# Attention scores by residue: near keys dense, far keys by position mod 4, two heads side by side in plain float32 products

## The chip, the cores and the metric

The kernel runs on one core of one Trainium2 chip. The metric is the device time of one execution in microseconds (us). The kernel before took 1199.07 us, the median of three runs (1199.07 to 1199.63). A difference of less than about 0.2% can't be told from none.

## What is computed

One layer of a decoder trunk: RMSNorm, one input projection, eight attention heads (this document's subject) and four HGRN2 heads side by side, an output projection, then a gated MLP with a short convolution, and a last RMSNorm. The sequence has 1024 positions, the model 1024 columns, an attention head 64. The part that the change touches:

```python
DILATED_PATTERNS = ((128, 1), (512, 4), (2048, 16))   # (window, dilation)

def dilated_attention(q, k, v):
    ...
    for window, dilation in DILATED_PATTERNS:
        o, m, l = dilated_branch(q, k, v, window, dilation)   # causal, keys at distance 0, d, 2d, ... up to window
        ...
    w = jnp.exp(ms - jnp.max(ms, axis=0, keepdims=True))
    den = jnp.sum(w * ls, axis=0)
    num = jnp.sum(w[..., None] * os_, axis=0)
    return (num / den[..., None])[:, :S]
```

The three branches are merged by their softmax denominators. So the whole is one softmax over the causal keys, in which a key counts as often as it stands in a branch: once for each distance up to 128, once more for each distance up to 512 that 4 divides, once more for each distance up to 2048 that 16 divides. Both kernels add the logarithm of that count to the score as a mask, and minus a huge number where the count is zero. Beyond a distance of 128 only distances that 4 divides have a count.

## The kernel before

**Number forms.** Most products run in a rounded float32 form (`F32R`). For accuracy the kernel splits an operand into a high part, rounded, and a low part, the rest, and adds up high x high, high x low and low x high: the dense projections are three products each. A weight piece of 128 x 512 comes by DMA on SP's queue (`Ring.fill`, line 66), ACT makes the high part (line 86), POOL or DVE the low part (line 88). The ring holds five split pieces and five raw ones.

**Stages.** First the norm sums and the projections of heads 0 and 1 and of the first values; then the attention stage, a loop over the heads; then HGRN, output projection, MLP. The attention stage does more than attention: a queue of other work (`Fill`, the projections of q and k of the next heads, of values and of HGRN's `iv`) is run in shares between the attention steps, by the microseconds that each step is said to cost. PE's instructions stand in the order in which the program writes them. The order on the other engines and in SP's DMA queue is made by a scheduler.

**Scores** (`score_steps`). For a head and a block of 128 queries, all causal keys: `n = 128 * (block + 1)` columns. The 64 numbers of a head fill half of the array's 128 rows, so the high part of q stands in rows 0 to 63 and its low part in rows 64 to 127 (`qs`), over the high part of k twice (`kh`); a second product with the low part of k (`kl`) over the high part of q completes it (lines 599, 600). `qk_half` makes `qs`, `kh` and `kl` out of the projection, for most heads by five SBUF-to-SBUF DMAs (line 568). DVE adds the mask and takes the row's minimum of the negated score (line 604), ACT takes the exponential and its sum (608), DVE the reciprocal (609), POOL scales (612).

**Values** (`value_steps`). Each 128 x 128 block of probabilities is transposed on TensorE (lines 627 to 634, tile `T`), split into a high part by ACT (637) and a low part by DVE (638), and multiplied with values that hold high and low parts side by side (646 to 650, tile `O`). An ACT copy and two DVE additions gather the output (654 to 657).

HGRN, later in the kernel, has a product that uses half of the array's columns (`psA`, lines 909 and 910): for a block of 128 positions the two chunks of 64 go to rows 0 to 63 and 64 to 127 of one PSUM bank, as plain float32 products.

Of the kernel before, what the change touches and what calls it, by code (L numbers as in the profile page):

```python
# [43 lines left out]
def f32(ap):  # L44
    return ap.bitcast(F32)
# [157 lines left out]
def hybrid_kernel(ctx: ExitStack, tc: tile.TileContext, xT, w_qk, w_tok, w_hg, w_out, w_up,  # L203
# [63 lines left out]
    want_tok("V1_0", 1)  # L267
    for h in (2, 3, 4):
        want(("qk", h), w_qk[h])
        want_tok(f"V1_{h - 1}", 1)  # L270
    want(("qk", 5), w_qk[5])
    want_iv(0)
    want(("qk", 6), w_qk[6])
    want_iv(1)
    want(("qk", 7), w_qk[7])
    want_iv(2)
    want_iv(3)
# [91 lines left out]
    TB = 3  # L369
# [156 lines left out]
    vs = {}  # L526
    iv = None
    if True:
        mask = at.tile([P, SEQ], F32, name="mask")
        nc.sync.dma_start(mask, amask)  # L530

        for hf in range(2):
            POOL.tensor_scalar(mask[:, halves[hf]], mask[:, halves[hf]], DH ** 0.5, 0.0, op0=ALU.mult, op1=ALU.add)
        NQ = 2
        kls = []
        for i in range(NQ):
            kl = at.tile([P, SEQ], F32R, name=f"kl{i}")
            POOL.memset(f32(kl[64:128]), 0.0)
            kls.append(kl)
# [3 lines left out]

        def qk_half(h, hf, last, tag="mm"):
            t = halves[hf]

            def evac(ps):
                if hf == 0:
                    qk[h] = (at.tile([P, SEQ], F32R, tag="qs", name=f"qs{h}", bufs=NQ),
                             at.tile([P, SEQ], F32R, tag="kh", name=f"kh{h}", bufs=NQ), kls[h % NQ])  # L550
                qs, kh, kl = qk[h]
                lo = at.tile([P, H2], F32R, tag="x", name=f"x{h}_{hf}")
                x = f32(lo)
                DVE.tensor_mul(x, ps, R1[:, t])
                if h == 0:
                    ACT.copy(qs[0:64, t], x[0:64])
                    ACT.copy(kh[64:128, t], x[64:128])
                    ACT.copy(kh[0:64, t], x[64:128])
                    DVE.tensor_sub(qs[64:128, t], x[0:64], f32(qs[0:64, t]))
                    DVE.tensor_sub(kl[0:64, t], x[64:128], f32(kh[64:128, t]))  # L560
                    return

                hi = at.tile([P, H2], F32R, tag="xh", name=f"xh{h}_{hf}")
                ACT.copy(hi, x)
                DVE.tensor_sub(lo, x, f32(hi))
                for dst, src in ((qs[0:64, t], hi[0:64]), (kh[64:128, t], hi[64:128]), (kh[0:64, t], hi[64:128]),
                                 (qs[64:128, t], lo[0:64]), (kl[0:64, t], lo[64:128])):
                    nc.sync.dma_start(f32(dst), f32(src))
            return dense(("qk", h), hf, evac, last, tag)
# [3 lines left out]

        def v_evac(g):
            def evac(t, ps):
                if g not in vs:
                    vs[g] = vtile([P, 8, 4, P], F32R, f"v{g}")
                dst = vs[g][:, t]
                src = ps[:, :256].rearrange("p (h e) -> p h e", h=4)
                ACT.mul(dst[:, :, 0:64], src, R1T[:, t : t + 1])  # L580
                DVE.scalar_tensor_tensor(dst[:, :, 64:128], src, R1T[:, t : t + 1], f32(dst[:, :, 0:64]),
                                         op0=ALU.mult, op1=ALU.subtract)
            return evac

        def score_steps(h, j):
            Ps = []
            qs, kh, kl = qk[h]
            for i in range(2):
                qb = 2 * j + i
                n = (qb + 1) * P  # L590
                Pt = at.tile([P, (5 + i + 2 * (j % 2)) * P], F32, tag=f"P{j % 2}{i}", name=f"P{h}_{qb}")
                st = at.tile([P, 16], F32, tag="st", name=f"st{h}_{qb}", bufs=8)
                Ps.append(Pt)
                cut = 320 if n == 640 else H2
                for k0 in range(0, n, cut):
                    w = min(n, k0 + cut) - k0
                    S = bank("s", f"S{h}_{qb}_{k0}")
                    q = qs[:, qb * P : (qb + 1) * P]
                    PE.matmul(S[:, :w], q, kh[:, k0 : k0 + w], start=True, stop=False)  # L599
                    PE.matmul(S[:, :w], q, kl[:, k0 : k0 + w], start=False, stop=True)  # L600
                    m = SEQ - n + k0

                    low = st[:, k0 // cut : k0 // cut + 1]
                    DVE.tensor_tensor_reduce(Pt[:, k0 : k0 + w], S[:, :w], mask[:, m : m + w], -(DH ** -0.5),  # L604
                                             st[:, 0:1] if k0 else BIG * 3,
                                             op0=ALU.add, op1=ALU.min, accum_out=low)
                    if k0 + w == n:
                        ACT.activation(Pt[:, :n], Pt[:, :n], AF.Exp, bias=low, scale=-1.0, accum_out=st[:, 2:3])  # L608
                        DVE.reciprocal(st[:, 3:4], st[:, 2:3])  # L609
                        for s0 in range(0, n, H2):  # L610
                            e = Pt[:, s0 : min(n, s0 + H2)]
                            POOL.tensor_scalar(e, e, st[:, 3:4], 1.0, op0=ALU.mult, op1=ALU.mult)  # L612
# [938 lines left out]
```

## Time and profile before

| | |
|---|---|
| median of the runs | 1199.07 us |
| span of the profiled execution | 1197.7 us |
| PE busy | 1186.0 us, 99% of the span |
| DVE busy | 938.7 us, 78% |
| ACT busy | 621.1 us, 52% |
| POOL busy | 300.4 us, 25% |
| first score product of attention | 40.1 us |
| first product of HGRN | 290.66 us |

The profile is of one execution; its span, from the first to the last instruction, is what sums are made against, and its median run time is 1.4 us above it. A timeline row gives start, duration, engine, line, operation, output and inputs, the part of the array used (rows * columns), the shape, and a count; matmuls overlap, so their durations are longer than their pitch. A row of groups gives the count, busy time and mean duration, and the idle time before it with what ended it. In the row of a stretch the busy times of PE, weight loads (PEld), DVE, ACT and POOL stand one after the other.

### The profile page before, as it was taken

Reading aid. Unit: us, or ns where it says so; the run is one execution under the profiler, and the core shown is the slowest. Engines: PE = TensorE matmul, PEld = TensorE weight load, DVE = VectorE, ACT = ScalarE, POOL = GpSimd, SP = SyncE. Lnnn points to the kernel's source line nnn. Section 1 sums busy time; section 2 is a strip of 40 time slices with the busy share of each in tenths; the row PEclk is TensorE's granted clock in tenths of the full one; section 3 lists DMA queues with packets and bytes.
Section 4 is the critical chain, followed back from the end, with each engine's and each line's share of the span. In section 5 each row is a group of like instructions: output and inputs, shape, how many; then the busy total and the mean of one; then the engine's idle time right before and its main releaser. Section 6 shows DMA issues by size and latency. Waiting matters only on the chain.

```text
span 1197.7 us, 17305 instructions
## 1 busy us (share of the span) xinstructions
PE 1186.0 (99%) x5854; PEld 995.9 (83%) x5854; DVE 938.7 (78%) x1762; ACT 621.1 (52%) x1203; POOL 300.4 (25%) x275
## 2 busy tenths in 40 slices
PE   9999999999999999999999999999999999999996
PEld 8988888888888888888888888888888888888886
DVE  7777675567878776485999889898888978957996
ACT  8666666667766554455543334343343444444553
POOL 2155446653001024322232222322232200000000
PEclk9999999999999999999999999999999999999998
DMA  7233333433102113441113322333223267435532
GB/s 264 53 96 103 100 104 104 133 105 100 48 33 62 60 57 120 138 140 60 53 62 114 118 80 98 119 115 121 87 92 115 97 234 238 153 97 157 169 104 91
DMA packets 77433, 131.56 MB, mean 110 GB/s; under 512 B 8480, under 2 KB 18976, under 8 KB 77344
## 3 DMA queue, kind: packets, MB, share of 16 engines
q1 hardware_dynamic: 66128, 110.59, 29.5%
q10 hardware_dynamic: 11216, 19.86, 4.3%
q8 instruction: 46, 0.75, 0.3%
q14 instruction: 43, 0.35, 0.1%
HBM read 97.65 MB, written 23.59 MB: 101 GB/s over the span
## 4 chain that ended last, share of the span: by engine, by line
PE 98%; DVE 1%; DMA 0%; POOL 0%; issue 0%; SPq 0%; ACT 0%; DVEq 0%
PE p L1152 11%; PE p L1150 11%; PE p L1151 11%; PE ds L1450 3%; PE ds L1449 3%; PE ds L1451 3%; PE po L1054 2%; PE po L1056 2%; PE po L1055 2%; PE da L1450 2%; PE da L1451 2%; PE da L1449 2%; PE O L646 2%; PE S L600 1%; PE S L599 1%; PE piv L513 1%
## 5 line engine op out<-in xcount | busy, mean ns | idle before, releaser
L88 POOL TENSOR_TENSOR wlo<-raww,whi 128x512 fp32r<-128x512 f32 x138 | 205.6, 1500 | 371.6 <-ACT whi L86 258.3
L86 ACT CAST whi<-raww 128x512 fp32r<-128x512 f32 x276 | 167.8, 617 | 191.7 <-DVE raww L120 62.1
L88 DVE TENSOR_TENSOR wlo<-raww,whi 128x512 fp32r<-128x512 f32 x139 | 99.1, 714 | 20.2 <-ACT whi L86 20.1
L86 ACT CAST whi<-r 128x512 fp32r<-128x512 f32 x70 | 43.6, 622 | 81.0 <-PE ds L1450 48.1
L612 POOL TENSOR_SCALAR P<-P,st 128x512 f32<-128x512 f32 (+2 forms) x96 | 57.9, 612 | 96.1 <-DVE st L609 76.9
L638 DVE TENSOR_TENSOR t<-T,t 128x512 fp32r<-128x512 f32 (+1 forms) x80 | 50.9, 636 | 17.5 <-ACT t L637 16.1
L88 DVE TENSOR_TENSOR wlo<-r,whi 128x512 fp32r<-128x512 f32 x70 | 48.2, 690 | 18.8 <-ACT whi L86 18.5
L1451 PE MATMUL ds<-fhi,wlo 128*128 128x512 f32 x160 | 62.2, 389 | 0.0
L1150 PE MATMUL p<-b1h,whi 128*128 128x512 f32 x160 | 62.2, 389 | 0.0
L1151 PE MATMUL p<-b1l,whi 128*128 128x512 f32 x160 | 62.2, 389 | 0.0
L1152 PE MATMUL p<-b1h,wlo 128*128 128x512 f32 x160 | 62.2, 389 | 0.0
L1449 PE MATMUL ds<-fhi,whi 128*128 128x512 f32 x160 | 62.2, 389 | 0.0
L1450 PE MATMUL ds<-flo,whi 128*128 128x512 f32 x160 | 62.2, 389 | 0.0
L608 ACT ACTIVATE P<-P,st 128x128 f32<-128x128 f32 (+3 forms) x64 | 49.7, 777 | 23.8 <-DVE st L604 23.2
L1179 ACT ACTIVATE cv<-cv 128x512 f32<-128x512 f32 x44 | 27.8, 632 | 62.0 <-DVE cv L1172 61.9
L1172 DVE SCALAR_TENSOR_TENSOR cv<-g,vec,cv 128x511 f32<-128x511 f32 (+2 forms) x92 | 56.1, 616 | 4.7 <-ACT cv L1169 3.7
L637 ACT CAST t<-T 128x512 fp32r<-128x512 f32 (+1 forms) x80 | 43.2, 540 | 29.5 <-PE T L631 26.4
L1423 POOL TENSOR_TENSOR facc<-facc,sqf 128x256 f32<-128x256 f32 x2 | 1.5, 738 | 223.6 <-ACT sqf L1422 223.6
L604 DVE CUSTOM_DVE_ANT_0 P<-S,mask 128x128 f32<-128x128 f32 (+3 forms) x64 | 35.5, 562 | 27.2 <-PE S L600 21.0
L88 DVE TENSOR_TENSOR flo<-rawf,fhi 128x512 fp32r<-128x512 f32 x70 | 48.3, 689 | 3.3 <-ACT fhi L86 3.2
L86 ACT CAST fhi<-rawf 128x512 fp32r<-128x512 f32 x70 | 43.2, 617 | 14.0 <-PE p L1152 5.0
L1449 PE MATMUL da<-fhi,whi 128*128 128x512 f32 x120 | 46.7, 389 | 0.0
(677 smaller groups left out, 3774.3 us busy)
## 6 DMA issues: line engine op xcount, KB each, us to landing
raww<-in_w_up_dram SPq DMA_DIRECT2D x88, 256.0 KB, 3.0
raww<-in_w_tok_dram SPq DMA_DIRECT2D x52, 256.0 KB, 2.8
rawf<-spT SPq DMA_DIRECT2D x40, 256.0 KB, 2.7
r<-in_w_down_dram SPq DMA_DIRECT2D x40, 256.0 KB, 3.4
raww<-in_w_hg_dram SPq DMA_DIRECT2D x32, 256.0 KB, 2.6
raww<-in_w_out_dram SPq DMA_DIRECT2D x32, 256.0 KB, 2.6
spB<-a ACTq DMA_DIRECT2D x30, 256.0 KB, 2.2
spT<-t ACTq DMA_DIRECT2D x30, 256.0 KB, 2.0
```

What stands on the lines that cost most here:

```text
L86: self.pin(self.high(hi[:, :w], raw))
L88: self.pin(low.tensor_sub(lo[:, :w], raw, f32(hi[:, :w])))
L608: ACT.activation(Pt[:, :n], Pt[:, :n], AF.Exp, bias=low, scale=-1.0, accum_out=st[:, 2:3])
L612: POOL.tensor_scalar(e, e, st[:, 3:4], 1.0, op0=ALU.mult, op1=ALU.mult)
L638: DVE.tensor_sub(t2[:, 1, :n], T[:, :n], f32(t2[:, 0, :n]))
L1150: PE.matmul(ps, hi[:, s], bhi, start=(start and n == 0), stop=False)
L1151: PE.matmul(ps, hi[:, s], blo, start=False, stop=False)
L1152: PE.matmul(ps, lo[:, s], bhi, start=False, stop=(stop and n == len(rhs) - 1))
L1172: DVE.scalar_tensor_tensor(dst, x, col(V_CW + j * NFF + f), dst, op0=ALU.mult, op1=ALU.add)
L1449: PE.matmul(ps[d], hi[:, s], ahi, start=(k == 0), stop=False)
L1450: PE.matmul(ps[d], hi[:, s], alo, start=False, stop=False)
L1451: PE.matmul(ps[d], lo[:, s], ahi, start=False, stop=(k == NPAIR - 1))
```

## The change

Three things change together, for the attention stage alone.

**Keys.** A block of 128 queries is now scored against near keys (its own block and the one before, at most 256 columns, dense) and far keys (all blocks before these). The queries of a block are stored in the order of their residue mod 4, 32 of each (`by_residue`); the 32 queries of residue r are scored against the far keys of residue r alone, read at a stride of four: four products of 32 queries by `32 * block` columns, which go to four groups of 32 PSUM rows. Far keys of other residues have a count of zero. A score row is thus at most 480 columns, where it was 1024. The mask is made anew in this order (`sel`, `scratch`, `mask`: POOL keeps each key either in the near or in the far part, and two trips through DRAM put the rows in the order of the residues).

**Number form and heads.** q, k, v and the probabilities are no longer split: the products are plain float32. Two heads stand side by side, head 2p in rows 0 to 63 and head 2p + 1 in rows 64 to 127 of `qp` and `kp`, and their products use half of the array's rows each, with a PSUM bank for each head. In the value products the heads use half of the array's columns each and go to the two halves of one bank.

**Values and order.** Values are kept once (`V`) for the near keys; they are also written to DRAM (`vd`), from where `load_far` reads them by residue for the far keys. The far probabilities are collected over a half of the sequence: `far_t` for the keys that all four blocks of the second half share, `tri` for the others. The loop runs over four pairs of heads and eight blocks: scores of the next block, a share of the fill, the transposes of this block, another share; after four blocks the value products. The ring's plan has the weights in the matching order.

```diff
-    for h in (2, 3, 4):
+    for h in (2, 3):
         want(("qk", h), w_qk[h])
-        want_tok(f"V1_{h - 1}", 1)
...
+    for i in (0, 1):
+        want_tok(f"V1_{i}", 1)
...
     def aside(i):
-        t = at.tile([P, 2, H2], F32R, tag="t", name=f"tw{i}", bufs=TB)
+        t = at.tile([P, 2, H2], F32R, tag="k0", name=f"tw{i}", bufs=2)
...
+        FAR, NEAR = 224, 256
+        nat = at.tile([P, SEQ], F32, tag="k0", name="nat", bufs=2)
...
+        nc.sync.dma_start(nat1[:, 0:NEAR], amask[:, SEQ - NEAR :])
+        nc.sync.dma_start(nat[0:32, 0:896], amask[0:P:4, 0:896])
...
+        nc.sync.dma_start(scratch[:, FAR:], sel[:, FAR:])
+        nc.sync.dma_start(scratch[0:32, 0:FAR], sel[0:32, 0:FAR])
+        for r in range(4):
+            nc.sync.dma_start(mask[32 * r : 32 * r + 32, FAR:], scratch[r:P:4, FAR:])
+            nc.sync.dma_start(mask[32 * r : 32 * r + 32, 0:FAR], scratch[0:32, 0:FAR])
...
+        def by_residue(ap):
+            return ap.rearrange("p (b l r) -> p b r l", l=32, r=4)
...
+                q4 = qp[r0 : r0 + 64, t].rearrange("p (b r l) -> p b r l", r=4, l=32)
+                DVE.tensor_mul(q4, by_residue(ps[0:64]), by_residue(R1[0:64, t]))
+                DVE.tensor_mul(kp[r0 : r0 + 64, t], ps[64:128], R1[64:128, t])
...
+                dst = V[:, t, 4 * g : 4 * g + 4]
+                ACT.mul(dst, ps[:, :256].rearrange("p (h e) -> p h e", h=4), R1T[:, t : t + 1])
+                nc.scalar.dma_start(vd[t * P : (t + 1) * P, 256 * g : 256 * g + 256], dst)
...
+        def load_far(p, kb):
...
+            src = vd[H2 * kb : H2 * (kb + 1), P * p : P * (p + 1)]
+            nc.sync.dma_start(far_v[p][:, kb], src.rearrange("(p r) e -> p r e", r=4))
...
+        def scores(p, b):
...
+            for e in range(2):
+                PE.matmul(S[e][:, far:n], qp[rows[e], b * P : (b + 1) * P], kp[rows[e], k0 : k0 + near],
+                          start=True, stop=True)
+            for r in range(4 if b else 0):
+                o = slice(32 * r, 32 * r + 32)
+                for e in range(2):
+                    PE.matmul(S[e][o, 0:far], qp[rows[e], b * P + 32 * r : b * P + 32 * r + 32],
+                              kp[rows[e], r : r + 4 * far : 4], start=True, stop=True)
...
+        def turn(p, b):
...
+                    PE.transpose(T[:, e, x], Ps[e][:, c : c + P], ident)
+            ACT.copy(d[:, :, x0:], T[:, :, x0:])
...
+                    PE.transpose(T[:, x, e], Ps[e][:, x * P : (x + 1) * P], ident)
...
+                DVE.tensor_copy(far_t[p][:, :, b - 4], T[:, 0])
...
+                DVE.tensor_copy(tri[b // 4][0:n, :, b % 4 - 1], T[0:n, parts - 1])
+
+        def values(p, hf):
...
+                        PE.matmul(O4[rows[e], i], V[:, b - 1 + x, 2 * p + e], t[:, e, x], start=(i == 0 and x == 1), stop=False)
...
+                        PE.matmul(O4[rows[e], :, q], v[:, 0, r, rows[e]], far_t[p][:, e, :, q], start=False, stop=False)
...
+                    PE.matmul(O4[rows[e], 1:, q], v[0:96, hf, r, rows[e]], tri[hf][0:96, e, :, q], start=False, stop=(r == 3))
...
+        for p in range(NH // 2):
+            work, us = beside[p]
+            fill.add(*work)
+            for b in range(8):
+                while ends:
+                    values(*ends.pop())
+                s = 8 * p + b + 1
+                if s < 32:
+                    scores(s // 8, s % 8)
+                fill.run(us / 16)
...
+                turn(p, b)
...
```

How the instructions move is seen at three places. The first is PE in the middle of the attention stage. Before, rows for block 3 of head 3 (`S` scores, `kh`/`kl` keys, `p__qk___4_0` a projection from the fill queue, `T` transposes):

```order
L599 MATMUL S_3_0_1756<-kh_1451,qs_1450 128x512
L600 MATMUL S_3_0_1756<-kl_206,qs_1450 128x512
L459 MATMUL p__qk___4_0_1747<-uhi,whi_1571 128x512
L461 MATMUL p__qk___4_0_1747<-ulo,whi_1571 128x512
L462 MATMUL p__qk___4_0_1747<-uhi,wlo_1572 128x512
L627 MATMUL T_0_0_1767<-ident,P_0_1605 128x128
L628 MATMUL T_0_0_1767<-ident,P_1_1617 128x128
L634 MATMUL T_0_0_1767<-ident,P_1_1617 128x128
```

In the changed program, block 3 of the second pair of heads (`S_3_0` and `S_3_1` are the two heads' banks):

```order
L460 MATMUL p__qk___4_1_1424<-uhi,whi_1266 128x512
L462 MATMUL p__qk___4_1_1424<-ulo,whi_1266 128x512
L463 MATMUL p__qk___4_1_1424<-uhi,wlo_1267 128x512
L610 MATMUL S_3_0_1457<-kp_840,qp_839 128x256
L610 MATMUL S_3_1_1458<-kp_840,qp_839 128x256
L615 MATMUL S_3_0_1457<-kp_840,qp_839 32x96
L615 MATMUL S_3_1_1458<-kp_840,qp_839 32x96
```

Two full-width products of one head have become two near products and eight far ones of two heads; the last two rows stand three more times, for the other residues. The second place is PE where value products stand. Before, one step of head 3:

```order
L646 MATMUL O_3_1629<-t_3_3_1695,v_439 128x512
L648 MATMUL O_3_1629<-t_3_3_1695,v_439 128x2x128
L459 MATMUL p__qk___4_1_1832<-uhi,whi_1571 128x512
L461 MATMUL p__qk___4_1_1832<-ulo,whi_1571 128x512
L462 MATMUL p__qk___4_1_1832<-uhi,wlo_1572 128x512
```

In the changed program, the first half of the first pair of heads (`pl` the transposed near probabilities, `vs` the values by residue):

```order
L669 MATMUL O_0_928<-pl_0_660,V 64x128 x2
L669 MATMUL O_0_928<-pl_1_758,V 64x128 x4
L669 MATMUL O_0_928<-pl_2_826,V 64x128 x4
L669 MATMUL O_0_928<-pl_3_897,V 64x128 x4
L676 MATMUL O_0_928<-tri_227,vs_548 64x3x32 x8
L610 MATMUL S_5_0_952<-kp_335,qp_334 128x256
L610 MATMUL S_5_1_953<-kp_335,qp_334 128x256
```

The value products, before spread between pieces of the fill, now stand together, with the scores of the next block right behind them. The third place is SP's DMA queue after the loads of x. Before:

```order
L530 DMA mask<-in_amask_dram 128x1024
L66 DMA raww_331<-in_w_tok_dram 128x512
L66 DMA raww_337<-in_w_tok_dram 128x512
L66 DMA raww_343<-in_w_tok_dram 128x512
L66 DMA raww_352<-in_w_tok_dram 128x512
```

In the changed program, from the load of the far mask on (`nat`; the near half has gone the same way a few rows ahead):

```order
L536 DMA nat<-in_amask_dram 32x896
L66 DMA raww_724<-in_w_qk_dram 128x512
L66 DMA raww_736<-in_w_qk_dram 128x512
L66 DMA raww_748<-in_w_qk_dram 128x512
L546 DMA scratch<-sel 32x224
L66 DMA raww_771<-in_w_tok_dram 128x512
L66 DMA raww_880<-in_w_tok_dram 128x512
L549 DMA mask<-scratch 32x224 x4
L596 DMA vs_548<-vd 128x4x128
L596 DMA vs_1160<-vd 128x4x128
L66 DMA raww_910<-in_w_tok_dram 128x512
L66 DMA raww_1042<-in_w_tok_dram 128x512
```

One load of the mask has become a chain through DRAM with weight loads in between, and the loads of the far values (`vs`) stand ahead of later weight loads. The five copies of each projected q and k half (line 568) are gone from the queue.

More of the change, by code (lines that the diff above doesn't have):

```diff
@@ L542, in hybrid_kernel @@
         qk = {}
+        def by_residue(ap):
+            return ap.rearrange("p (b l r) -> p b r l", l=32, r=4)
         def qk_half(h, hf, last, tag="mm"):
             t = halves[hf]
+            p, r0 = h // 2, 64 * (h % 2)
             def evac(ps):
[L548 to L568, printed above, removed]
+                if p not in qk:
+                    qk[p] = [at.tile([P, SEQ], F32, tag=x, name=f"{x}{p}", bufs=2) for x in ("qp", "kp")]
+                qp, kp = qk[p]
+                q4 = qp[r0 : r0 + 64, t].rearrange("p (b r l) -> p b r l", r=4, l=32)
+                DVE.tensor_mul(q4, by_residue(ps[0:64]), by_residue(R1[0:64, t]))
+                DVE.tensor_mul(kp[r0 : r0 + 64, t], ps[64:128], R1[64:128, t])
             return dense(("qk", h), hf, evac, last, tag)
@@ L572, in qk_block @@
             return [qk_half(h, 0, False), qk_half(h, 1, True)]
+        V = None
+        vd = drv.tile([SEQ, NH * DH], F32, name="vd")
         def v_evac(g):
             def evac(t, ps):
[L576 to L582, printed above, removed]
@@ L583, in v_evac @@
-            return evac
[L585 to L592, printed above, removed]
-                Ps.append(Pt)
[L594 to L612, printed above, removed]
-                    yield Ps
@@ L683, in iv_evac @@
             ACT.mul(iv[:, t], ps, R1T[:, t : t + 1])
-        lo4, hi4, all8 = range(4), range(4, 8), range(8)
+        all8 = range(8)
         v0 = [tok("V0", t, v_evac(0), t == 7, "mm" if t > 1 else "s") for t in all8]
@@ L709, in hybrid_kernel @@
         ring.on_vector += [(("out", 1, d), i) for d in range(NCT) for i in range(2)]
-        for Ps in score_steps(0, 0):
-            pass
+        scores(0, 0)
         fill.add(v0[3])
         fill.run()
+        load_far(0, 0)
         rms1(1)
@@ L719, in hybrid_kernel @@
         fill.run()
+        for g in pairs[1]:
+            next(g, None)
         ivs = [tok_pair(i, iv_evac) for i in range(4)]
[L721 to L730 removed]
@@ L764, in hybrid_kernel @@
-        while pending:
-            late_pv()
-        late_ends()
+        twos = [two("V1", i, v_evac(1)) for i in range(4)]
+        beside = [(v0[5:] + qk_block(2) + qk_block(3) + twos[:2], 39.3),
+                  (qk_block(4) + qk_block(5) + twos[2:], 31.4),
+                  (qk_block(6) + qk_block(7) + ivs[:1], 31.2),
+                  (ivs[1:], 31.2)]
+        ends = []
+        for p in range(NH // 2):
[8 more added lines that the diff above has]
+                fill.run(us / 16)
+                if b == 3:
+                    load_far(p, 1)
+                turn(p, b)
+                if b == 6 and p < 3:
+                    load_far(p + 1, 0)
+                if b == 7:
+                    fill.run()
+                else:
+                    fill.run(us / 16)
+                if b % 4 == 3:
+                    ends.append((p, b // 4))
@@ L767, in hybrid_kernel @@
+        values(*ends.pop())
+    drv_cm.__exit__(None, None, None)
     at_cm.__exit__(None, None, None)
```

201 lines of the change are left out of this document (84 added, 117 removed).

## The prediction

> **What bounds the kernel now.** I read first the page (shares of the span, then the chain that ended last), then the list of what TensorE (PE) waited for, then the busy time in the stretch that the change touches.
>
> ```profile
> span 1197.7 us, 17305 instructions
> ...
> PE 1186.0 (99%) x5854; PEld 995.9 (83%) x5854; DVE 938.7 (78%) x1762; ACT 621.1 (52%) x1203; POOL 300.4 (25%) x275
> ...
> PE 98%; DVE 1%; DMA 0%; POOL 0%; issue 0%; SPq 0%; ACT 0%; DVEq 0%
> ```
>
> PE is busy for 99% of the span and is 98% of the chain. The list of PE's waits in the whole execution is three rows long:
>
> ```profile
> PE T L628 <- POOL P L612: 1.1, 2, 0.7
> PE warm L382 <- DVE ones L229: 1.1, 1, 1.1
> PE p__qk___0_0_212 L459 <- ACT uhi L398: 0.3, 1, 0.3
> ```
>
> Only the first row, 1.1 us, is in the attention stage. The stage itself, from the last pieces before the loop over heads to the first HGRN product, reads so (PE, weight loads, DVE, ACT, POOL, each busy time with its count):
>
> ```profile
> 48.00:291.00 243.00, 241.90 (x1386) 209.25 (x1385) 162.91 (x443) 160.26 (x337) 128.11 (x151) 1.00 0.36 102
> ```
>
> PE has no gap, at granted clock 1.00; the next engine, DVE, is busy 163 of 243 us. So the stage lasts as long as PE's instructions take one after the other, and the change is worth what it does to that sum, unless it makes PE wait. A row's duration is no measure of that, since matmuls overlap; what counts is the pitch, from one start to the next.
>
> **What attention costs PE before.** The counts come from the score row and the value rows, the pitches from PE's timeline (start, duration).
>
> ```profile
> L600 PE MATMUL S<-kl,qs x96: 274/337/402, 40.3 to 275.9; 128*128 128x512 f32 x40, 128*128 128x256 f32 x16, 128*128 128x384 f32 x16, 128*128 128x320 f32 x16
> L646 PE MATMUL O<-t,v 128*128 128x512 f32 x80 | 32.4, 405 | 0.0
> L650 PE MATMUL O<-t,v 128*128 128x512 f32 x48 | 18.9, 393 | 0.0
> L648 PE MATMUL O<-t,v 128*128 128x256 f32 x32 | 8.9, 279 | 0.0
> ...
> 48.20 0.34 PE L599 MATMUL S<-kh,qs 128*128 128x384 f32 x1
> 48.38 0.34 PE L600 MATMUL S<-kl,qs 128*128 128x384 f32 x1
> ...
> 57.16 0.27 PE L627 MATMUL T<-ident,P 128*128 128x128 f32 x1
> 57.27 0.27 PE L628 MATMUL T<-ident,P 128*128 128x128 f32 x1
> ...
> 58.20 0.40 PE L646 MATMUL O<-t,v 128*128 128x512 f32 x1
> 58.43 0.28 PE L648 MATMUL O<-t,v 128*128 128x256 f32 x1
> 58.55 0.28 PE L476 MATMUL pV<-whi,uhi 128*128 128x256 f32 x1
> ```
>
> Pitches: 0.107 us a transpose, 0.233 for 512 columns in the split type, 0.12 for 256, 0.18 for 384, and 0.15 for 320 by interpolation. L599 has the same forms as L600, and each line has 8 of 128 columns that the row leaves out. Scores: 80 x 0.233 + 32 x 0.18 + 32 x 0.15 + 32 x 0.12 + 16 x 0.12 = 35.0 us. Transposes: 36 key blocks for each of 8 heads, 288 x 0.107 = 30.8. Values: 128 x 0.233 + 32 x 0.12 = 33.6. Together **99.4 us**, and 1.1 us of waiting. The rest of the stage (projections that the fill queue puts between) stays as it is, only regrouped.
>
> **What attention costs PE after.** Its products are plain float32, and half or a quarter of the array wide. The trace has both things, in other places: a plain product over the whole array (the sum of squares) and pairs of plain products that each fill 64 of the 128 columns (psA of HGRN).
>
> ```profile
> 23.00 1.02 PE L414 MATMUL ss<-sq,ones 128*128 128x512 f32 x2
> 23.86 0.95 PE L417 MATMUL sst<-ones,sq 128*128 128x1 f32 x8
> ...
> 318.88 0.39 PE L462 MATMUL p__hg___0_1_3862<-uhi,wlo 128*128 128x512 f32 x1
> 319.11 0.60 PE L904 MATMUL psK<-ident,B 128*128 128x128 f32 x4
> 319.63 0.32 PE L909 MATMUL psA<-E,B 128*64 128x128 f32 x1
> 319.64 0.32 PE L910 MATMUL psA<-E,B 128*64 128x128 f32 x1
> 319.79 0.27 PE L909 MATMUL psA<-E,B 128*64 128x128 f32 x1
> 319.80 0.27 PE L910 MATMUL psA<-E,B 128*64 128x128 f32 x1
> ...
> 320.45 0.27 PE L909 MATMUL psA<-E,B 128*64 128x128 f32 x1
> 320.45 0.27 PE L910 MATMUL psA<-E,B 128*64 128x128 f32 x1
> 320.66 0.50 PE L459 MATMUL p__hg___0_1_3862<-uhi,whi 128*128 128x512 f32 x1
> 320.99 0.40 PE L461 MATMUL p__hg___0_1_3862<-ulo,whi 128*128 128x512 f32 x1
> ```
>
> Three prices follow. A plain product stands as two instructions and takes 23.86 - 23.00 = 0.86 us for 512 columns, 1.68 ns a column. Two half-wide products start 10 ns apart and move on together: a pair of 128 columns takes two slots of 0.108 us, 0.217, where one after the other it would take 0.43. And since the program gives both instructions of L909 before those of L910, but the trace starts one of each together, a tile doesn't wait in line behind its neighbour. Third, a change of tile shape isn't free: from the end of the transposes (319.11 + 4 x 0.107 = 319.54) to 320.99 are 1.45 us, of which 8 slots are 0.87 and the 512-column product 0.23; 0.35 is left for two changes of shape, **0.175 each**.
>
> Now the parts. *Transposes*: per pair of heads 30 near and 20 far blocks, 200 in all, 200 x 0.107 = 21.4 us. *Near scores*: 28 blocks with two products of 256 columns and 4 with two of 128. If the two heads' halves (64 rows each) run side by side, 28 x 0.43 + 4 x 0.215 = 12.9; if not, 25.8. The trace shows halves of columns beside each other, not halves of rows; I take 12.9, since the rows of array that a tile uses are apart in the same way. *Far scores*: per block 8 products of 32 to 224 columns, 28,672 columns in all: 48.2 us one after the other, 24.1 if two run together, 6.0 if all eight tiles do. Eight short products are 16 weight loads and 16 matmuls; the densest stretch above carries four such instructions in 0.108 us, and at that rate 32 take 0.87 us a block, 24 us in 28 blocks, whatever the tiles do. That rate was set by the array there, so it is an upper bound of issue. Between 6.0 and 24.1 I take **16**, nearer the middle than either, as long blocks are bound by columns and short ones by issue. *Values*: 60 near pairs and 16 far pairs of 128 columns at 0.217, 32 pairs of 96 columns at 0.163: 16.5 + 5.2 = 21.7; this is the psA case itself, and 43.4 if it failed. *Changes of shape*: the program has 101 of them in attention (near, far, and back, 28 times; the value blocks stand directly ahead of scores): 17.7 us; half of that if the drain is shorter where a small weight load follows.
>
> Sum: 21.4 + 12.9 + 16 + 21.7 + 17.7 = **89.7 us** against 99.4.
>
> For the far products the Trainium skill, page "TensorE: Matmul & The Clock Gate", section "Part 3: Packing small matmuls — row/col tiling", gives 3.07 times for four row tiles and 10.6 times for sixteen, with short gaps between tiles. An estimate from it for eight tiles, between these, would be about 48.2 / 6 = 8 us, and the sum 8 us lower than mine. No run here shows it yet, and its products are long where these are short.
>
> **What must not make PE wait.** *DVE, ACT, POOL* get less. ACT and DVE lose the two parts of each transposed block, the ACT copy and two DVE adds per output block, and a third of the score columns; they gain 32 near copies, 40 far copies and 8 output copies. With these rows
>
> ```profile
> L638 DVE TENSOR_TENSOR t<-T,t 128x512 fp32r<-128x512 f32 (+1 forms) x80 | 50.9, 636 | 17.5 <-ACT t L637 16.1
> L637 ACT CAST t<-T 128x512 fp32r<-128x512 f32 (+1 forms) x80 | 43.2, 540 | 29.5 <-PE T L631 26.4
> L604 DVE CUSTOM_DVE_ANT_0 P<-S,mask 128x128 f32<-128x128 f32 (+3 forms) x64 | 35.5, 562 | 27.2 <-PE S L600 21.0
> L608 ACT ACTIVATE P<-P,st 128x128 f32<-128x128 f32 (+3 forms) x64 | 49.7, 777 | 23.8 <-DVE st L604 23.2
> L612 POOL TENSOR_SCALAR P<-P,st 128x512 f32<-128x512 f32 (+2 forms) x96 | 57.9, 612 | 96.1 <-DVE st L609 76.9
> L88 POOL TENSOR_TENSOR wlo<-raww,whi 128x512 fp32r<-128x512 f32 x138 | 205.6, 1500 | 371.6 <-ACT whi L86 258.3
> ```
>
> DVE sheds 50.9 us and gets back some 48 copies at about 0.5, ACT sheds 43.2 and gets back 32 at about 0.54. *A block's own chain*: from its last score product to its transposes PE has three shares of fill (31.2/16 us each at least), the transposes of the block before and the scores of the block after, 5.9 + 0.6 + 1.5 = 8 us. The chain is two reductions (1.1 to 1.4), exp (two of 0.78), reciprocal, scaling (0.6 each): about 4 us. Behind two weight splits of 1.5 us on POOL it is 7, still inside. Without that cover each block would cost the excess. *The mask* comes in two loads that pass through DRAM, and V goes out to DRAM and comes back for the far keys. What they hang on, in the time before:
>
> ```profile
> 25.92 0.39 PE L462 MATMUL p__qk___1_1_273<-uhi,tw 128*128 128x512 f32 x1
> ...
> 43.79 0.47 ACT L580 ACTIVATE v<-pV,R1T 128x256 fp32r<-128x256 f32 x1 [1.37 <-PE pV L478]
> ...
> r<-in_w_down_dram SPq DMA_DIRECT2D x40, 256.0 KB, 3.4
> ...
> spT<-t ACTq DMA_DIRECT2D x30, 256.0 KB, 2.0
> ```
>
> The far mask is loaded into the buffer of head 1's first weights, which ends with the fourth chunk of eight, at 26 us; three DMA legs of 2 to 3.4 us and two POOL steps bring it to at most 40, and the block that needs it first stands near 48 (the row at 48.20 above). *load_far(0, 0)* waits on SP for V of four blocks: 44.3 and a store of 2 us. Behind it on SP stand weight loads for V1, which are now used only after the projections of the next two heads (4 x 24 products x 0.233 = 22 us of fill). I cost all of that at 0.5 us; without that cover PE would wait a whole load, 2 to 3 us, once each.
>
> So the stage goes from 99.4 + 1.1 to 89.7 + 0.5: 10.3 us less. The span of the profiled execution, 1197.7, becomes 1187.4; the median of the runs is 1.4 above that span, so the forecast is **1189 us**. With the bounds of the far scores (6 to 24) and of the shape changes (half to once and a half) this case's own range is 1177 to 1198.
>
> **Rivals.**
> *The far products go no faster than pairs, or are bound by issue.* 24.1 in place of 16: 1197. For it speaks that they are short; against it, that psA's instructions overtook each other. Chance 0.15.
> *Reading each fourth column halves the stream.* The far keys are read at a stride of four floats, which no matmul of the trace does. If each column takes twice as long, 16 becomes 32, and the time 1205. Chance 0.08. The Trainium skill has such a rule: "Advanced Engine Details and Errata", section "SBUF Cachelines", says that full rate needs two hits in each 16-byte line, and here there is one; a plain product that visits its moving data more than once may not feel it, and no row shows it.
> *Row halves don't run side by side.* Near scores 25.8, far scores 24.1 (four column tiles would still overlap) to 48.2: 12.9 + 8.1 = 21 us more than the sum, 1210, or 1234 at the far end. Nothing in the trace excludes it, since every tiled product there uses all 128 rows. It decides from the point where near and far scores together pass 39 us. Chance 0.12.
> *PE waits for the block's chain.* If POOL runs its weight splits ahead of the scaling in most blocks, and PE stands 0.5 us in each of 32 blocks, 16 us come back: 1205. Against it: PE waited twice in the whole stage before, with more work on the others. Chance 0.05.
>
> **How the numbers follow.** The forecast's case has 0.60. A difference below 0.2%, 2.4 us, can't be told from none. Faster: nearly all of the forecast's case and half of the pair case, 0.65. Same: the other half, a little of the first and last, 0.13. Slower: the row case, the stride case and the waits, 0.22. The range is 1177 to 1206: it leaves out the row case and the best corner of the first.
>
> **What would show it.** After the change the two heads' near products should start within some 20 ns of each other and advance 0.21 us a step; if the second starts after the first has ended, the row rival holds. The eight far products of a block should take 0.3 to 0.9 us; 1.5 us at the longest block means pairs, 3 means none. Around each scores group some 0.5 us should go to the changes of shape. The list of PE's waits should stay under 2 us in the stage, and the stage's first HGRN product should start near 281 in place of 290.7. The forecast is wrong if PE shows gaps before the transposes, or if the far group takes more than 24 us in all.

## The result and the profile after

The changed kernel takes 1186.24 us (median of 4 runs, 1185.77 to 1186.35), against 1199.21 us for the kernel before beside it. The ratio is 0.9892, with a 95% interval of 0.9878 to 0.9906: 13.0 us, or 1.1%, faster. The profiled execution has a span of 1184.6 us, 13.1 less than before.

The page of the changed kernel: busy time of each engine with its count of instructions, then the shares of the chain that ended last.

```profile
span 1184.6 us, 17883 instructions
...
PE 1174.0 (99%) x6422; PEld 964.1 (81%) x6422; DVE 866.8 (73%) x1585; ACT 563.3 (48%) x1103; POOL 277.1 (23%) x244
...
PE 98%; DVE 1%; DMA 0%; POOL 0%; ACT 0%; SPq 0%; issue 0%; DVEq 0%; POOLq 0%
```

TensorE (PE) still sets the end, with 568 instructions more and 12 us less of busy time. What it waited for, in the whole execution:

```profile
PE warm L383 <- DVE ones L229: 1.1, 1, 1.1
PE p__qk___1_0_250 L460 <- ACT tw L86: 0.2, 1, 0.2
```

Neither row is in the attention stage; the 1.1 us before the transposes is gone. The same stretch as before, 48 to 291 us, with the busy time of PE, weight loads, DVE, ACT and POOL:

```profile
48.00:291.00 243.00, 242.94 (x2012) 188.88 (x2010) 102.51 (x295) 111.09 (x255) 105.38 (x118) 1.00 0.28 87
```

DVE went from 163 to 103 us, ACT from 160 to 111, POOL from 128 to 105, and none of that is worth anything by itself, since PE had but 1.1 us of waiting there before. (The last 13 us of the stretch now belong to HGRN.) The gain shows at the stretch's end. PE's timeline of the last value products and of the first HGRN product behind them:

```profile
274.26 1.97 PE L669 MATMUL O<-pl,V 128*64 128x128 f32 x32
276.05 0.39 PE L674 MATMUL O<-k,vs 128*64 128x128 f32 x4
...
277.70 0.50 PE L460 MATMUL p__hf___0_0_3186<-uhi,whi 128*128 128x512 f32 x1
```

and the row of the kernel before for the same place:

```profile
290.66 0.40 PE L459 MATMUL p__hf___0_0_3608<-uhi,whi 128*128 128x512 f32 x1
```

The first HGRN product starts 12.96 us earlier, and the span is 13.1 us shorter: all of it was won in this stage, and the rest of the program kept it. Keys, number form and order changed together, and no run takes them apart; what each of them is worth rests on sums alone.

**How the scores run.** PE's timeline at block 1 and block 7 of the first pair, with the fill behind, and for block 7 also the fill ahead:

```profile
48.43 0.70 PE L610 MATMUL S<-kp,qp 64*128 64x256 f32 x4
49.06 0.33 PE L615 MATMUL S<-kp,qp 64*32 64x32 f32 x16
49.32 0.38 PE L477 MATMUL pV<-whi,uhi 128*128 128x256 f32 x1
...
94.26 0.28 PE L496 MATMUL pV<-whi,ulo 128*128 128x256 f32 x1
94.47 0.70 PE L610 MATMUL S<-kp,qp 64*128 64x256 f32 x4
95.10 1.00 PE L615 MATMUL S<-kp,qp 64*32 64x224 f32 x16
96.03 0.39 PE L494 MATMUL pV<-whi,uhi 128*128 128x256 f32 x1
96.25 0.28 PE L495 MATMUL pV<-wlo,uhi 128*128 128x256 f32 x1
```

Starts are to be compared, not durations. From the near products to the far products it is 0.63 us in both blocks. From the far products to the fill it is 49.32 - 49.06 = 0.26 us at 32 far columns and 96.03 - 95.10 = 0.93 us at 224: 0.67 / 6 = **0.112 us for each 32 columns** of the eight far products. One such product alone, at the 1.68 ns a column of the prediction, would take 0.054 us. One after the other the eight would take 0.43. So either all eight run at once at half their rate, or four at a time at full rate.

The records of single instructions show the first. In block 7 of the last pair the two heads' near products start 6 ns apart, at 262.488 and 262.494. The eight far products start within 47 ns, from 263.120 to 263.167, all of them before the second instruction of any. Those second instructions begin 0.384 us later; at the rate above, half of a 224-column product would be 0.19. The near products' second instructions begin 0.320 us after the first and the far products 0.312 us after those, where 256 columns in half a product are 0.215.

The group's length gives the changes of shape. From the end of the fill (94.26 + 0.12) to the near products it is 0.09 us. The near products take 0.63, where 256 columns at 1.68 ns are 0.43: 0.20 too much. Behind the far products (0.93, of which 7 x 0.112 are columns) 0.15 is left, and the first fill product takes 0.22 in place of 0.12. That is 0.09 + 0.20 + 0.15 + 0.10 = **0.54 us a group**.

### The profile page after: what moved, and what is told of

Same layout as the page of the kernel before. It is cut to its first block, busy times and chain, and to the rows that moved or that the text cites. A ratio compares the mean times of both kernels' runs of the same rounds, so it can differ in the third digit from the quotient of the medians.

```text
span 1184.6 us, 17883 instructions
## 1 busy us (share of the span) xinstructions
PE 1174.0 (99%) x6422; PEld 964.1 (81%) x6422; DVE 866.8 (73%) x1585; ACT 563.3 (48%) x1103; POOL 277.1 (23%) x244
## 4 chain that ended last, share of the span: by engine, by line
PE 98%; DVE 1%; DMA 0%; POOL 0%; ACT 0%; SPq 0%; issue 0%; DVEq 0%; POOLq 0%
PE p L1136 11%; PE p L1137 11%; PE p L1138 11%; PE ds L1437 3%; PE ds L1435 3%; PE ds L1436 3%; PE po L1040 2%; PE po L1042 2%; PE po L1041 2%; PE da L1437 2%; PE da L1435 2%; PE da L1436 2%; PE S L610 2%; PE S L615 1%; PE piv L514 1%; PE piv L516 1%
## 5 line engine op out<-in xcount | busy, mean ns | idle before, releaser
L622 DVE CUSTOM_DVE_ANT_0 P<-S,mask 128x128 f32<-128x128 f32 (+7 forms) x64 | 31.2, 522 | 63.9 <-PE S L615 54.3
L624 ACT ACTIVATE P<-P,st 128x128 f32<-128x128 f32 (+7 forms) x64 | 37.2, 583 | 78.3 <-DVE st L622 78.2
L88 DVE TENSOR_TENSOR wlo<-r,whi 128x512 fp32r<-128x512 f32 x70 | 48.2, 690 | 19.0 <-ACT whi L86 19.0
L626 POOL TENSOR_SCALAR P<-P,st 128x128 f32<-128x128 f32 (+7 forms) x64 | 35.7, 559 | 108.7 <-DVE st L625 103.0
L88 DVE TENSOR_TENSOR flo<-rawf,fhi 128x512 fp32r<-128x512 f32 x70 | 48.2, 689 | 4.0 <-ACT fhi L86 4.0
L1436 PE MATMUL da<-flo,whi 128*128 128x512 f32 x120 | 46.7, 389 | 0.0
L1437 PE MATMUL da<-fhi,wlo 128*128 128x512 f32 x120 | 46.7, 389 | 0.0
```

Of the source, the lines that this page charges most:

```text
L88: self.pin(low.tensor_sub(lo[:, :w], raw, f32(hi[:, :w])))
L622: DVE.tensor_tensor_reduce(Pt[:, :n], S[e][:, :n], m, -(DH ** -0.5), BIG * 3, op0=ALU.add, op1=ALU.min, accum_out=st[:, 0:1])
L624: ACT.activation(Pt[:, :n], Pt[:, :n], AF.Exp, bias=st[:, 0:1], scale=-1.0, accum_out=st[:, 2:3])
L626: POOL.tensor_scalar(Pt[:, :n], Pt[:, :n], st[:, 3:4], 1.0, op0=ALU.mult, op1=ALU.mult)
L1436: PE.matmul(ps[d], hi[:, s], alo, start=False, stop=False)
L1437: PE.matmul(ps[d], lo[:, s], ahi, start=False, stop=(k == NPAIR - 1))
```

## Experiments

The forecast came out within its range, 2.8 us above the time. What was open: whether the half rate of the far products comes from the stride of four floats or from the array rows that four tiles share, what the row halves are worth, and whether the block's chain is hidden by the cover that the prediction named. From the answers a better version followed.

### The far keys read in a row

Only the address of the far keys changes; the far scores are then those of other keys, with the same count of products, columns and weights.

```diff
-                              kp[rows[e], r : r + 4 * far : 4], start=True, stop=True)
+                              kp[rows[e], 32 * r : 32 * r + far], start=True, stop=True)
```

> The changed kernel with one edit: the far products read 32*b keys in a row in place of each fourth one (so the far scores are those of wrong keys; nothing else is left out). In the changed kernel a far group grows by 0.113 us for each 32 columns, where eight tiles side by side at the full rate of a plain product would need 0.054. Theory 'stride' (each fourth float costs a second slot): the growth falls to 0.054 us, the group of scores of block 7 from 1.76 to about 1.38 us, and the time by 28 x 4 x 0.057 = 6.4 us, to 1180. Theory 'shared rows' (four tiles of columns that read the same 64 rows get half the rate whatever they read): nothing moves, 1186.

Measured: 1180.0 us, ratio to the kernel before 0.9835 (0.982 to 0.9849), 6.2 us under the changed kernel. PE's timeline at block 7:

```profile
93.28 0.70 PE L610 MATMUL S<-kp,qp 64*128 64x256 f32 x4
93.91 0.61 PE L615 MATMUL S<-kp,qp 64*32 64x224 f32 x16
94.45 0.39 PE L494 MATMUL pV<-whi,uhi 128*128 128x256 f32 x1
```

The far products now take 94.45 - 93.91 = 0.54 us in place of 0.93. Over the blocks the far products grow by 0.053 us for each 32 columns, which is the full rate of a single product. So the half rate comes from the stride, and eight tiles that share rows four by four lose nothing. By it 4 x 28 x (0.112 - 0.053) = 6.6 us were to be had; the span fell by 6.5. That the two agree so closely is in part chance: the score and value groups themselves are 5.9 us shorter, since a group takes some 0.02 us more beside its columns here, and the rest lies in the fill products between the groups.

### A stride of two floats

```diff
-                              kp[rows[e], r : r + 4 * far : 4], start=True, stop=True)
+                              kp[rows[e], r : r + 2 * far : 2], start=True, stop=True)
```

> The changed kernel with the far products reading each second key in place of each fourth (so the far scores are those of wrong keys). Theory 'two floats of a 16-byte line are enough' (the rule that the prediction cited): full rate, 0.054 us for each 32 columns as with keys in a row, 1180. Theory 'any stride costs': 0.113 us as with a stride of four, 1186.

Measured: 1179.92 us, ratio 0.9838 (0.9818 to 0.9857). PE's timeline at block 7:

```profile
92.61 0.70 PE L610 MATMUL S<-kp,qp 64*128 64x256 f32 x4
93.25 0.64 PE L615 MATMUL S<-kp,qp 64*32 64x224 f32 x16
93.81 0.39 PE L494 MATMUL pV<-whi,uhi 128*128 128x256 f32 x1
```

0.56 us, and 0.057 us for each 32 columns: a stride of two costs next to nothing, a stride of four doubles the time. The Trainium skill's page "Advanced Engine Details and Errata", section "SBUF Cachelines", asks for two hits in each 16-byte line. Stride two gives two hits, stride four one, and the trace agrees on both sides, with 0.057 and 0.112 us.

### Both heads on the same rows of the array

The second head's products read rows 0 to 63 as the first head's do. Its own scores are left out, and those of the first head stand in their place.

```diff
-                PE.matmul(S[e][:, far:n], qp[rows[e], b * P : (b + 1) * P], kp[rows[e], k0 : k0 + near],
+                PE.matmul(S[e][:, far:n], qp[rows[0], b * P : (b + 1) * P], kp[rows[0], k0 : k0 + near],
...
-                    PE.matmul(S[e][o, 0:far], qp[rows[e], b * P + 32 * r : b * P + 32 * r + 32],
-                              kp[rows[e], r : r + 4 * far : 4], start=True, stop=True)
+                    PE.matmul(S[e][o, 0:far], qp[rows[0], b * P + 32 * r : b * P + 32 * r + 32],
+                              kp[rows[0], r : r + 4 * far : 4], start=True, stop=True)
```

> The changed kernel with one edit: the score products of both heads of a pair read rows 0 to 63, so the second head's scores are the first's and its own are left out. It takes away what two row halves of the array give. Theory of the prediction (the halves run side by side): near products go from 0.43 to 0.86 us a block (+12.9 us in all) and far groups from 0.113 to 0.226 us for each 32 columns (+12.7), some 25 us more, 1211, all of it on PE, with the second near product starting 0.43 us after the first. Rival (something else sets the pace of a group, such as issue): less than 10 us more.

Measured: 1211.41 us, ratio 1.0098 (1.0077 to 1.0118). PE's timeline at block 7:

```profile
99.89 1.13 PE L610 MATMUL S<-kp,qp 64*128 64x256 f32 x4
100.94 1.79 PE L615 MATMUL S<-kp,qp 64*32 64x224 f32 x16
102.66 0.39 PE L494 MATMUL pV<-whi,uhi 128*128 128x256 f32 x1
```

The near products take 1.05 us in place of 0.63, the far products 1.72 in place of 0.93. Over all blocks that is 28 x 0.42 + 4 x 0.21 + 4 x 28 x 0.112 = 25.1 us, and the run is 25.2 longer. That the two halves of rows run side by side is therefore worth 25 us, twice the whole gain. Had it failed, the change would have been 12 us slower.

### Near scores in the far products' shape

Four products of 32 queries for each head replace one of 128. The same scores are computed, and the change of shape between near and far products goes away.

```diff
-            for e in range(2):
-                PE.matmul(S[e][:, far:n], qp[rows[e], b * P : (b + 1) * P], kp[rows[e], k0 : k0 + near],
-                          start=True, stop=True)
+            for r in range(4):
+                o = slice(32 * r, 32 * r + 32)
+                for e in range(2):
+                    PE.matmul(S[e][o, far:n], qp[rows[e], b * P + 32 * r : b * P + 32 * r + 32],
+                              kp[rows[e], k0 : k0 + near], start=True, stop=True)
```

> The changed kernel with one edit: the near scores too are made in four products of 32 queries for each head, in the tile shape of the far ones, so that one change of shape falls away in 28 blocks; it computes the same. Theory 'stride': the near keys stand in a row, so eight tiles take the 0.43 us that two took, and the time falls by the change of shape, 28 x 0.11 = 3 us, to 1183. Theory 'shared rows': the near group doubles to 0.86 us, 28 x 0.43 + 4 x 0.21 = 12.9 us more, less 3: 1196.

Measured: 1181.26 us, ratio 0.9847 (0.9831 to 0.9864), 5.0 us under the changed kernel. PE's timeline at block 7:

```profile
93.51 0.66 PE L612 MATMUL S<-kp,qp 64*32 64x256 f32 x16
93.96 0.99 PE L617 MATMUL S<-kp,qp 64*32 64x224 f32 x16
94.89 0.39 PE L494 MATMUL pV<-whi,uhi 128*128 128x256 f32 x1
```

From near to far it is 0.45 us in place of 0.63, which is the 0.43 of the columns and nothing more. Sixteen instructions take no longer than the four did, since eight tiles run at once; 28 x 0.18 = 5.0 us is the whole gain. I had put it at 3 us, from the change between near and far alone. The records of single instructions show two equal parts. The step from the near products' second instructions to the far products is 0.216 us, where it was 0.312: that is the change of shape. And the step from their first to their second instructions is 0.240 us, where it was 0.320. So the first products behind a change of shape run longer by 0.105 us with 128 columns of weights and by 0.025 with 32. The weight loads of these products differ by the same 0.08 us: 0.184 with 128 columns, 0.105 with 32. It looks like the load of a second set of weights that nothing hides, but no run takes that apart.

### The scores of a block only one share of fill ahead

The loop gives a block's scores in the same turn as its transposes, no longer one turn ahead. The same is computed.

```diff
-                s = 8 * p + b + 1
-                if s < 32:
-                    scores(s // 8, s % 8)
+                if p or b:
+                    scores(p, b)
```

> The changed kernel with one edit: a block's scores are made one share of fill (about 2.1 us) ahead of its transposes in place of three shares and another block's work (about 8 us). It computes the same. The prediction put the chain from the last score product to the scaled probabilities at about 4 us, and so hidden. If so, PE now waits some 2 us in each of 31 blocks for POOL's scaling: about 60 us more, 1245. If the chain is as long as the cover (8 us), 180 us more; if it is under 2 us, nothing.

Measured: 1210.59 us, ratio 1.0091 (1.0071 to 1.0111), 24.4 us over the changed kernel, or 0.76 us a block. The list of PE's waits names the place:

```profile
PE Tn L641 <- POOL P L626: 11.5, 31, 1.4
```

The 11.5 us is only the time in which no matmul was still counted as busy; counted from start to start, the steps up to and among the transposes are 23.5 us longer than in the changed kernel, nearly the whole loss. The timeline of block 1 of the third pair shows the chain (the bracket gives the idle time ahead of an instruction and what ended it):

```profile
184.82 0.33 PE L615 MATMUL S<-kp,qp 64*32 64x32 f32 x16
185.34 0.46 DVE L622 CUSTOM_DVE_ANT_0 P<-S,mask 128x288 f32<-128x288 f32 x1 [4.01 <-PE S L615]
185.85 0.54 ACT L624 ACTIVATE P<-P,st 128x288 f32<-128x288 f32 x1 [3.25 <-DVE st L622]
186.51 0.16 DVE L625 RECIPROCAL st<-st 128x1 f32<-128x1 f32 x1 [0.32 <-ACT P L624]
186.76 0.50 POOL L626 TENSOR_SCALAR P<-P,st 128x288 f32<-128x288 f32 x1 [4.96 <-DVE st L625]
186.77 1.06 DVE L570 TENSOR_TENSOR qp<-p__qk___6_0_1969,R 64x512 f32<-64x512 f32 x1
...
187.32 0.44 PE L641 MATMUL Tn<-ident,P 128*128 128x128 f32 x2
187.76 0.15 DVE L625 RECIPROCAL st<-st 128x1 f32<-128x1 f32 x1
...
188.00 0.50 POOL L626 TENSOR_SCALAR P<-P,st 128x288 f32<-128x288 f32 x1 [0.73 <-DVE st L625]
...
188.56 0.44 PE L641 MATMUL Tn<-ident,P 128*128 128x128 f32 x2 [0.80 <-POOL P L626]
```

The first head's probabilities are there 187.32 - 185.08 = 2.2 us after the far products (185.08 is where the fill follows them), the second head's 3.5 us after. In this block the second head came late because DVE ran a 1.06 us evacuation of the projections ahead of its reciprocal. I had expected some 1245 us from a chain of 4 us; the chain is shorter, since the two heads overlap on three engines and PE begins with the first head's transposes. Over the 32 blocks of this run the second head's probabilities are there 2.1 to 4.3 us after the scores, half of them within 3.1. But the chain is longer than one share of fill, so the cover that the order gives is needed: it is worth 24 us.

### The keys kept a second time, in the order of residues

If the stride costs 6.6 us, the keys can be stored so that the far products read them in a row. DVE writes them a second time when it evacuates the projections. The space comes from fewer buffers elsewhere (near probabilities, far probabilities, far values). The same is computed.

```diff
+                k4 = kr[r0 : r0 + 64].rearrange("p (r b l) -> p b r l", r=4, l=32)[:, 4 * hf : 4 * hf + 4]
+                DVE.tensor_mul(k4, by_residue(ps[64:128]), by_residue(R1[64:128, t]))
...
-                              kp[rows[e], r : r + 4 * far : 4], start=True, stop=True)
+                              kr[rows[e], 256 * r : 256 * r + far], start=True, stop=True)
```

> The changed kernel with k kept a second time, in the order of the residues (one more DVE product of 64 x 512 per projected half, some 1.1 us each, 16 in all), so that the far products read the right keys without a stride; to make room the far probabilities, the transposed near ones and the far values have fewer buffers. It computes the same. Theory 'stride': as with the far keys in a row, 1180, if DVE (103 of 243 us busy in the stage) still has room and the fewer buffers make nobody wait. Theory 'the gain is eaten': PE waits appear for DVE or for a buffer, and the time stays near 1186.

Measured: 1182.12 us, ratio 0.986 (0.9845 to 0.9875): 4.1 us under the changed kernel, 2 less than reading in a row was worth. The list of PE's waits:

```profile
PE piv L514 <- DVE kr L573: 0.6, 1, 0.6
PE S L611 <- DVE st L623: 0.5, 1, 0.5
PE pV L494 <- DVE kr L573: 0.3, 1, 0.3
```

New waits have come in, two for the new DVE product itself and one for a reduction (`st`); the group of block 2 takes 2.25 us where it took 1.10 with the keys read in a row.

### The same with near scores in the far shape

> The same, with the near scores also in four products of 32 queries: both edits together. It computes the same. If the two gains are of different things (the stride 6.2 us, the change of shape 5.0 us), they add up: 1175. If the second gain was part of the first, 1180. The group of scores of block 7 should take 0.43 + 0.38 + two changes of shape of 0.36 in all, some 1.18 us.

This puts the two edits together. Measured: 1176.94 us, ratio 0.9814 (0.9798 to 0.9831). The gains add: 5.2 us below the run with the second copy alone, where the near scores' edit alone gave 5.0. Block 7's group takes 1.17 us as expected, but block 2's still takes 2.11 where 0.90 was due. DVE's timeline ahead of it:

```profile
49.87 1.07 DVE L570 TENSOR_TENSOR qp<-p__qk___0_1_293,R 64x512 f32<-64x512 f32 x1
50.95 0.69 DVE L571 TENSOR_TENSOR kp<-p__qk___0_1_293,R 64x512 f32<-64x512 f32 x1
51.57 1.07 DVE L573 TENSOR_TENSOR kr<-p__qk___0_1_293,R 64x512 f32<-64x512 f32 x1
52.65 1.08 DVE L570 TENSOR_TENSOR qp<-p__qk___1_1_297,R 64x512 f32<-64x512 f32 x1
...
54.36 1.05 DVE L573 TENSOR_TENSOR kr<-p__qk___1_1_297,R 64x512 f32<-64x512 f32 x1
...
55.64 0.46 DVE L625 CUSTOM_DVE_ANT_0 P<-S,mask 128x288 f32<-128x288 f32 x1
```

Six evacuations stand in a row ahead of the second reduction of block 1 (55.64), and the score banks come free only behind it. The two `kr` rows are 2.1 us of that. DVE is busy for less than half of the stage (107.7 of the 220 us from 48 to 268), and yet late here.

### The second copy made by ACT

```diff
-                DVE.tensor_mul(k4, by_residue(ps[64:128]), by_residue(R1[64:128, t]))
+                ACT.copy(k4, by_residue(kp[r0 : r0 + 64, t]))
```

> The kernel with k kept twice and near scores in quarters, but the second copy of k is made by ACT out of the first one in place of a DVE product out of PSUM. It computes the same. In that kernel (1176.9) DVE stood with six products in a row, 5.6 us, ahead of the second reduction of block 1 of the first pair, and the scores of block 2 took 2.11 us in place of 0.90. If this queue is where 2 us went, they come back: 1175. If ACT's exponentials now wait behind the copies and PE for them, no gain, 1177 or more.

Measured: **1173.95 us**, ratio 0.9788 (0.9771 to 0.9804), the best of all: 2.1% under the kernel before, 12.3 us under the changed kernel. The list of PE's waits and block 7 on PE's timeline:

```profile
PE warm L383 <- DVE ones L229: 1.0, 1, 1.0
```

```profile
91.68 0.66 PE L613 MATMUL S<-kp,qp 64*32 64x256 f32 x16
92.14 0.58 PE L618 MATMUL S<-kr,qp 64*32 64x224 f32 x16
92.65 0.39 PE L494 MATMUL pV<-whi,uhi 128*128 128x256 f32 x1
```

With the copy on ACT no wait is left in the stage, block 2's group takes the 0.90 us that were due, and 3 us come back. The buffers are as few as in the two runs before, so it was DVE's queue and not the buffers that held PE there. Block 7's scores go from 96.03 - 94.47 = 1.56 us to 0.97. The score and value groups together take 53.2 us in place of 65.0, which is 11.8 of the 12.6 us that the span fell. Of the other 0.8, 0.3 lie ahead of the first scores, which start at 40.01 in place of 40.34; the rest I did not place.

## Why the prediction was right, step by step

**The bound.** Right: PE has next to no gap in the stage (1.1 us before, none after), and the change was worth what it did to the sum of PE's instructions. From the prediction's 100.5 us for the kernel before, the sum goes to 87.0 as measured, 13.5 less; the stage's end moved by 12.96.

| term | predicted, us | measured, us |
|---|---|---|
| transposes, 200 | 21.4 | 21.4 (same instructions, not measured apart) |
| near scores | 12.9 | 12.9 |
| far scores | 16 | 12.5 |
| values | 21.7 | 21.7 |
| changes of shape | 17.7 | 18.5 (what is left) |
| waits | 0.5 | 0 |
| sum | 90.2 | 87.0 |

All score and value groups together, from the end of a fill product to the start of the next, with the 0.10 us by which that next one is longer, come to 65.0 us, and 0.6 for the first scores ahead of the stage: 65.6 with the far columns, the near ones, the values and the changes of shape in it. The last near values, sixteen products in eight pairs, take 276.05 - 274.26 = 1.79 us, where 8 x 0.217 are 1.74. The changes of shape are what is left: 28 times 0.54 or 0.55, 0.40 at each of the four first blocks, and 1.6 in all at the value groups.

**Where it was off.** One step was mis-sized, the far scores: "Between 6.0 and 24.1 I take 16". They took 4 x 28 x 0.112 = 12.5 us. Two things were wrong in it, in opposite senses. First, the eight tiles do all run at once; the far products read in a row take 4 x 28 x 0.053 = 5.9 us, the lower bound of 6.0. Nothing of an issue bound is to be seen: the group of block 1, with 16 short products, is explained by its columns and its changes of shape (0.43 + 0.05 + 0.54 = 1.02 us in the run that reads in a row, measured 1.05). Second, the stride does double the time. I had that as a rival, at 0.08, and priced it on top of 16 us; its mechanism is right, and it doubles 5.9 to 12.5. The argument held against it, that a plain product which visits its data more than once may not feel the stride, fell. That the forecast came so near the time is therefore in part luck: no row stood behind the 16 itself, a point chosen between two bounds, and what it missed on one side the stride took back on the other. With the keys in a row that term would have been 10 us too high.

The estimate from the Trainium skill's page "TensorE: Matmul & The Clock Gate", section "Part 3: Packing small matmuls — row/col tiling", was 8 us for eight tiles. Read in a row they took 5.9, a speed-up of 8 and not of 6; with the stride, 12.5.

**The range.** The bounds that the prediction names, 10 us below and 8 above for the far scores and 8.9 either way for the changes of shape, reach together from 1170 to 1206. The 1177 to 1198 that it calls its own range are not that sum.

**The rivals.** Pairs or issue (1197): no, as shown. Stride of four: the mechanism, yes, but not the price or the time that hung on it. Row halves one after the other (1210 to 1234): no; the near products start 6 ns apart. The run that forces it came to 1211, near the price of 1210 that the prediction gave, but not by its sum. For the far scores it took 24.1 us, "four column tiles would still overlap"; four at once would be 48.2 / 4 = 12.1, and the price some 1198. In the run four do overlap, and the stride, which the sum leaves out, turns the 12 into 25. PE waits for the chain (1205): no wait in the stage. The chain was put at 4 us, and at 7 behind two weight splits. In the changed kernel the second head's probabilities come 2.1 to 6.4 us after the scores, half of them within 3.1, so always inside the cover of 8 us; that cover was named rightly, and against one share of fill it is worth 24 us.

**The signs.** Near products within 20 ns of each other: 6 ns. That they advance 0.21 us a step: no, 0.32 and 0.31, since the change ahead and the change behind each put 0.10 on a step; side by side they run all the same. The far group between 0.3 and 0.9 us: 0.26 to 0.93. Half a microsecond for changes of shape: 0.54. The first HGRN product near 281 (290.7 less 10.3 is 280.4): 277.70, earlier by 2.7 us, for the most part the 3.5 us of the far scores.

**The chances.** The gain was real by five times the 2.4 us that count as a difference. Of the 0.35 that I gave to "same" and "slower", most hung on the row halves and the stride. The first was worth that: 25 us stood on it, and no row of the trace before showed it.

## What to carry to other kernels

Before a product is cut into small tiles, look at how its moving data is read: a stride of four floats halved the rate of eight tiles at once, 6.6 us here, and a second copy of the data in reading order, made by an engine with nothing urgent behind it, gave it back. Give neighbouring groups one tile shape, even where that needs four times the instructions, since the changes of shape cost more than the instructions did. Ask of each added piece of work what stands behind it on that engine: the same copy cost PE a wait on DVE, which was busy for less than half of the stage, and none on ACT, which with the copy was busy for 120 of 217 us. The share of busy time did not tell which engine could take it.

## What the runs showed of the hardware that I had not expected

- Eight plain float32 products of 64 rows by 32 columns of weights, with eight separate places in the array, start within 47 ns of each other, and together take as long as one (0.053 us for each 32 columns). The first instruction of the eighth starts before the second instruction of the first, though the two instructions of a product follow each other in the program: where a wait stops block 2's group after its first product (the second copy made by DVE, near scores in the far shape), both of that product's instructions, at 54.955 and 55.194, stand ahead of the wait, and the next one starts at 56.165.
- Their moving data at a stride of two floats costs 0.057 us for each 32 columns, at a stride of four 0.112.
- A group of products in another tile shape costs PE some 0.54 us beside its columns where near and far products have two shapes, and 0.36 where they have one.
- A DVE product of 64 x 512 that reads its two sources in the order of the residues, each fourth float, takes 1.05 to 1.08 us, where the same size read in a row takes 0.69 (`kr` and `qp` against `kp` in the rows above).
